# A block order for the value product and one shared tile for the top-k search in a hybrid attention trunk

## The chip, the cores and the metric

The kernel runs on one core of a Trainium2 chip. The metric is the device time of one execution in microseconds. TensorE (PE in the rows, its weight loads PEld) does the matrix products, VectorE (DVE) and ScalarE (ACT) the elementwise work, GpSimd (POOL) part of the copies and splits, SyncE (SP) issues most transfers.

## The reference

One layer over 1024 tokens of width 1024. After an RMS norm, one projection gives the inputs of three groups of heads, whose outputs are joined, multiplied by a SiLU gate, projected back, added to the input and normalised once more. Everything is float32.

```python
# A: differential attention, 6 heads, causal
p = softmax(where(causal, s, NEG)); a = p[:, :, 0] - lam * p[:, :, 1]
o_a = einsum('bhqk,bkhd->bqhd', a, v)
# B: sparse attention, 6 heads over one latent per key; per query the 256 best keys by an index score
rel = relu(einsum('bqhd,bsd->bqhs', iqb, ik))
score = where(causal, einsum('bqhs,bqh->bqs', rel, iwb) * IDX_SCALE, NEG)
_, sel = lax.top_k(score, 256)
o_lat = softmax(qlb . c_kv[sel]) . c_kv[sel];  o_b = einsum('bqhr,hrd->bqhd', o_lat, w_uv)
# C: retention, 4 heads, in chunks of 128
y = silu(gate) * concatenate([o_a, o_b, o_c]);  h = x + y @ w_out;  return rms_norm(h, final_norm)
```

## The kernel before

The 1024 queries are eight blocks of 128, and so are the keys. The work is written as generators that `run` interleaves by weights; within that, a scheduler sets each engine's order when the program is built, from a model of how long instructions take. Where the code stands in a `manual_schedule` block, it keeps the written order on the named engine. On the chip every engine works its queue in order.

The stages, with the times at which they lie in the trace: norm and transposes of x, the projection for keys and values and the index scores (to about 205 us, with TensorE's order written by hand at the end); then, interleaved, differential attention for three pairs of heads (`diff`, two heads each), the top-k search (`topk`) and the remaining projections as filler (to about 548 us); then sparse attention (`dsa`) for query blocks 0 to 3 (to about 612 us) and for blocks 4 to 7 (to about 760 us), with retention and the first output projections as filler; then the last output projections.

`attend` is the frame of `diff` and `dsa`. For each query block i it makes scores (L652 or L717 and L718), a softmax (L663 or L725 with the exponential L665 or L726 on ScalarE), transposes of the weights (L613) that ScalarE or VectorE copies out to the tile `pt` (L113, L117), and, when two query blocks are ready, one value product: a 128x128 result in PSUM whose lower 64 rows (u = 0) belong to query block i-1 and whose upper 64 (u = 1) to block i. Per key block k it is one matmul for each u, except that k = i has u = 1 alone (causal). So a group has 15, 11, 7 or 3 matmuls. There are 48 groups: 24 in differential attention, 12 in each half of sparse attention. A float32 matmul of this kind shows as two records in the trace. The tag "B" has two PSUM buffers, which the transposes and the value products share.

`topk` finds, for each query of blocks 2 to 7, the score that the 256th best key has, bit by bit: per bit, from 30 to 0, it counts how many scores reach a trial threshold. VectorE counts blocks 7, 4 and 2 (`gd`, line L372, with an accumulator), ScalarE blocks 6, 5 and 3 (`ga`, by the sum of a Sign activation, L388). The thresholds of each group stand in a tile of three columns (`tk_cd`, `tk_ca`), the counts in `tk_nd` and `tk_na`, a mask in `tk_md` and `tk_ma`. VectorE turns a count into the next threshold: two instructions for its own group (L394, L395), three for ScalarE's (L397 to L399). The two groups have no data in common until the end, where masks are made from the thresholds (L422 to L432) for sparse attention.

Of the kernel before, what the change touches and what calls it, by code (L numbers as in the profile page):

```python
# [68 lines left out]
class Trunk:  # L69
# [286 lines left out]
    def topk(self):  # L356
# [9 lines left out]
        st = {}  # L366
        thr = self.const("thr", [128, len(ga)])
        for j, b in enumerate(ga):
            nc.vector.memset(thr[:, j:j + 1], float(nv[b] - 2 * TOPK + 1))

        def count(b, t, op, cnt, bit=0):
            nc.vector.tensor_scalar(jv[:, :nv[b]], hb if b == 7 and bit >= 16 else sc[b], t, 0.0, op0=op, op1=OP.add, accum_out=cnt)  # L372

        for key, grp in (("d", gd), ("a", ga)):
            c = self.const("tk_c" + key, [128, len(grp)], I32)
            m = self.const("tk_m" + key, [128, len(grp)], I32)
            cnt = self.const("tk_n" + key, [128, len(grp)])
            st[key] = (c, m, cnt)
            for j, b in enumerate(grp):
                count(b, 0.0, OP.is_ge, cnt[:, j:j + 1])  # L380
            nc.vector.tensor_scalar(m, cnt, float(TOPK), -1.0, op0=OP.is_lt, op1=OP.mult)
            nc.vector.tensor_scalar(c, m, 1 << 30, None, op0=OP.bitwise_xor)
            yield 2.4
        for bit in range(30, -1, -1):
            nxt = (1 << bit) >> 1
            c, m, cnt = st["a"]
            for j, b in enumerate(ga):
                nc.scalar.activation(ja[:, :nv[b]], sc[b], AF.Sign, bias=c[:, j:j + 1].bitcast(F), scale=-1.0,  # L388
                                     accum_out=cnt[:, j:j + 1])
            yield 0.8  # L390
            c, m, cnt = st["d"]
            for j, b in enumerate(gd):
                count(b, c[:, j:j + 1].bitcast(F), OP.is_ge, cnt[:, j:j + 1], bit)
            nc.vector.tensor_scalar(m, cnt, float(TOPK), float(1 << bit), op0=OP.is_lt, op1=OP.mult)  # L394
            nc.vector.scalar_tensor_tensor(c, m, nxt, c, op0=OP.bitwise_xor, op1=OP.bitwise_xor)  # L395
            c, m, cnt = st["a"]
            nc.vector.tensor_tensor(cnt, cnt, thr, OP.is_gt)  # L397
            nc.vector.tensor_scalar(m, cnt, float(1 << bit), float(nxt), op0=OP.mult, op1=OP.add)
            nc.vector.tensor_tensor(c, m, c, OP.bitwise_xor)  # L399
            yield 1.6  # L400
        c, m, cnt = st["a"]
        w = self.const("tk_w", [128, 2, len(ga)])
        for j, b in enumerate(ga):
            count(b, c[:, j:j + 1].bitcast(F), OP.is_gt, cnt[:, j:j + 1])
        cf = c.bitcast(F)
        nc.vector.scalar_tensor_tensor(w[:, 0], cf, -1.0, cf, op0=OP.mult, op1=OP.max)
        nc.vector.tensor_scalar(w[:, 1], cnt, float(TOPK), 2.0 ** -24 * (1 + 2.0 ** -10), op0=OP.is_ge, op1=OP.mult)
# [6 lines left out]
        where = {b: (key, j) for key, grp in (("d", gd), ("a", ga)) for j, b in enumerate(grp)}  # L414
        for b in (7, 6, 5, 4, 3, 2):
            key, j = where[b]
            c, m, cnt = st[key]
            n, T = nv[b], c[:, j:j + 1].bitcast(F)
# [168 lines left out]
    def attend(self, pair, stages, GB=2, groups=(3, 2, 1, 0)):  # L587
# [8 lines left out]
        for t in range(N + 2):  # L596
# [22 lines left out]
            if t >= 2 and steps[t - 2][2] % GB == GB - 1:  # L619
# [354 lines left out]
```

## Time and profile before

| | |
|---|---|
| median of 3 runs | 814.09 us (812.97 to 814.19) |
| the profiled execution | 812.34 us |
| its span in the trace | 810.7 us |
| mean granted TensorE clock | 0.964 of full |
| TensorE, VectorE, ScalarE, GpSimd busy | 743.4, 568.7, 448.1, 332.9 us |
| value product, L627, busy | 78.3 us in 864 records |

Busy time is the time in which an engine has an instruction under way; the ends of matmuls are modelled, so a busy TensorE is not one at its peak, and start-to-start distances tell more than durations. Waits are put down to the engine whose event came last.

### The profile page before, as it was taken

How to read it: one execution, taken by the hardware profiler on the slowest of the kernel's cores; microseconds unless marked ns; L12 is line 12 of the kernel's file. 1: busy time of each engine (PE TensorE's matmuls, PEld its weight loads, DVE VectorE, ACT ScalarE, POOL GpSimd, SP SyncE). 2: the span in 40 equal slices, each digit the busy share in tenths (PEclk: the TensorE clock that was granted, in tenths of full speed). 3: DMA queues.
4: the chain of work that ended last, by engine and by line, in shares of the span. 5: the costliest groups of instructions: out<-in, count | busy, mean ns of one | idle time of the engine just before them, and what ended most of it. 6: DMA issues, size and time to landing. Idle time of an engine off the chain costs nothing.

```text
span 810.7 us, 12950 instructions
## 1 busy us (share of the span) xinstructions
PE 743.4 (92%) x4314; PEld 605.4 (75%) x4314; DVE 568.7 (70%) x1370; ACT 448.1 (55%) x998; POOL 332.9 (41%) x359
## 2 busy tenths in 40 slices
PE   3999999999999989989998789999778999999696
PEld 3798888888778878757876568988546887788584
DVE  5911377899999979999669998354646767653342
ACT  4521455558867857769876556441444656543232
POOL 6403222344424549348647896066745312110000
PEclk9999999999999999989998979999898999999798
DMA  9204644462473253261574573364579845211341
GB/s 331 65 1 106 195 125 145 131 162 84 123 195 101 70 150 109 80 160 34 137 234 143 151 210 116 95 216 144 175 240 300 225 133 166 77 60 59 126 149 59
DMA packets 93186, 113.05 MB, mean 139 GB/s; under 512 B 11840, under 2 KB 63424, under 8 KB 92992
## 3 DMA queue, kind: packets, MB, share of 16 engines
q1 hardware_dynamic: 91824, 109.61, 47.1%
q10 hardware_dynamic: 1296, 2.62, 0.9%
q8 instruction: 34, 0.56, 0.3%
q14 instruction: 32, 0.26, 0.1%
HBM read 75.50 MB, written 36.18 MB: 138 GB/s over the span
## 4 chain that ended last, share of the span: by engine, by line
PE 58%; DVE 23%; DMA 7%; issue 5%; POOL 3%; SPq 2%; ACT 1%; DVEq 0%; ACTq 0%; POOLq 0%
DVE jv L372 7%; PE pB L627 6%; PE pG L132 5%; PE pG L130 5%; PE pG L131 4%; PE pB L613 4%; PE pG L929 4%; PE pG L930 4%; PE pG L931 4%; PE pG L282 3%; PE pG L284 3%; PE pG L283 3%; DVE pp L681 2%; DVE pq L663 2%; PE pS L343 2%
## 5 line engine op out<-in xcount | busy, mean ns | idle before, releaser
L132 PE MATMUL pG<-uh,wl 128*128 128x512 f32 x352 | 143.2, 407 | 1.7 <-POOL wl L123 1.7
L130 PE MATMUL pG<-uh,wh 128*128 128x512 f32 x352 | 143.9, 409 | 0.5 <-POOL wh L119 0.5
L131 PE MATMUL pG<-ul,wh 128*128 128x512 f32 x352 | 143.0, 406 | 0.0
L123 POOL TENSOR_TENSOR wl<-wr,wh 128x512 fp32r<-128x512 f32 x56 | 81.2, 1468 | 115.3 <-PE pG L131 66.4
L388 ACT ACTIVATE ja<-sc,tk_ca 128x896 int8<-128x896 f32 (+2 forms) x93 | 83.3, 896 | 23.6 <-DVE tk_ca L399 9.7
L113 ACT ACTIVATE pt<-pB 128x512 f32<-128x512 f32 (+2 forms) x120 | 58.3, 495 | 56.1 <-PE pB L613 55.9
L613 PE MATMUL pB<-ident,pp 128*128 128x128 f32 x432 | 71.7, 283 | 11.5 <-DVE gt L755 5.4
L132 PEld LDWEIGHTS pG<-uh,wl 128*128 128x128 f32 x352 | 68.1, 194 | 18.1 <-POOL wl L123 2.7
L627 PE MATMUL pB<-pt,v 128*64 128x128 f32 x864 | 78.3, 284 | 2.6 <-ACT pt L113 2.5
L130 PEld LDWEIGHTS pG<-uh,wh 128*128 128x128 f32 x352 | 68.2, 194 | 15.3 <-issue 1.5
L131 PEld LDWEIGHTS pG<-ul,wh 128*128 128x128 f32 x352 | 68.0, 193 | 14.1 <-issue 0.7
L627 PEld LDWEIGHTS pB<-pt,v 128*64 128x64 f32 x864 | 58.8, 139 | 20.8 <-issue 9.1
L678 POOL TENSOR_SCALAR pq<-pq,mx 128x896 f32<-128x896 f32 (+7 forms) x48 | 44.2, 920 | 65.4 <-DVE mx L677 57.9
L613 PEld LDWEIGHTS pB<-ident,pp 128*128 128x128 f32 x432 | 50.7, 142 | 26.0 <-issue 6.5
L372 DVE TENSOR_SCALAR_CACHE_REDUCE jv<-sc,tk_cd 128x640 bf16<-128x640 f32 (+2 forms) x78 | 66.1, 847 | 0.5
L119 POOL TENSOR_SCALAR wh<-wr 128x512 fp32r<-128x512 f32 x56 | 43.4, 780 | 54.4 <-DMA wr<-in_w_in_dram 45.4
L929 PE MATMUL pG<-woh,yh 128*128 128x512 f32 x128 | 52.7, 412 | 11.1 <-ACT yh L113 11.1
L652 PE MATMUL pS<-st,st 128*128 128x512 f32 (+3 forms) x144 | 45.5, 380 | 13.2 <-DVE mx L663 7.0
L282 PE MATMUL pG<-wh,uh 128*128 128x256 f32 x192 | 55.8, 295 | 0.0
L283 PE MATMUL pG<-wl,uh 128*128 128x256 f32 x192 | 55.2, 289 | 0.0
L284 PE MATMUL pG<-wh,ul 128*128 128x256 f32 x192 | 55.0, 288 | 0.0
L345 ACT ACTIVATE pp<-pS 128x1024 f32<-128x1024 f32 (+5 forms) x48 | 36.5, 759 | 31.1 <-PE pS L343 30.5
(226 smaller groups left out, 1794.5 us busy)
## 6 DMA issues: line engine op xcount, KB each, us to landing
wr<-in_w_in_dram SPq DMA_DIRECT2D x56, 256.0 KB, 3.1
st<-qdq SPq DMA_DIRECT2D x24, 256.0 KB, 4.6
st<-qkk SPq DMA_DIRECT2D x18, 256.0 KB, 5.9
x<-in_x_dram SPq DMA_DIRECT2D x8, 512.0 KB, 6.6
qiq<-hl SPq DMA_DIRECT2D x16, 256.0 KB, 3.6
st<-qiq SPq DMA_DIRECT2D x8, 512.0 KB, 3.3
wr<-in_w_out_dram SPq DMA_DIRECT2D x16, 256.0 KB, 4.0
xr<-in_x_dram SPq DMA_DIRECT2D x8, 512.0 KB, 4.2
```

The lines of the kernel that those rows point to most:

```text
L123: (self.nc.vector if e2 == "v" else self.nc.gpsimd).tensor_tensor(lo, src, hi.bitcast(F), OP.subtract)
L130: mm(ps, wh, xh, start=start, stop=False)
L131: mm(ps, wh, xl, start=False, stop=False)
L132: mm(ps, wl, xh, start=False, stop=stop)
L282: mm(ps, uh, hs[k], start=k == 0, stop=False)
L283: mm(ps, uh, ls[k], start=False, stop=False)
L284: mm(ps, ul, hs[k], start=False, stop=k == KC - 1)
L372: nc.vector.tensor_scalar(jv[:, :nv[b]], hb if b == 7 and bit >= 16 else sc[b], t, 0.0, op0=op, op1=OP.add, accum_out=cnt)
L388: nc.scalar.activation(ja[:, :nv[b]], sc[b], AF.Sign, bias=c[:, j:j + 1].bitcast(F), scale=-1.0, accum_out=cnt[:, j:j + 1])
L613: nc.tensor.transpose(p[:, k], pr[:, (k0 + k) * 128:(k0 + k + 1) * 128], self.ident)
L627: nc.tensor.matmul(o[u * 64:(u + 1) * 64], self.v[:, k, h * 64:(h + 1) * 64], pts[g, a][:, k, u * 128:(u + 1) * 128], start=k == 0, stop=k ...
L929: mm(p, yh[:, k - c0], woh[:, k, ds], start=k == c0, stop=False)
```

## The change

Two edits. In `attend`, the matmuls of one value product are put into a `manual_schedule` block for TensorE, so that they keep the written order; that order begins with key block i (u = 1 alone) and goes on with k = 0 to i-1, upper half before lower half. The start and stop flags of the accumulation follow. In `topk`, one tile of six columns each holds all thresholds (`tk_c`), counts (`tk_n`) and masks (`tk_m`), VectorE's three blocks first. VectorE now counts scores below the threshold instead of at or above it, with a constant of its own per column (`thr`), so that the same three updates serve all six columns. Line numbers after the edits are three or four lower than before.

```diff
-        st = {}
-        thr = self.const("thr", [128, len(ga)])
-        for j, b in enumerate(ga):
-            nc.vector.memset(thr[:, j:j + 1], float(nv[b] - 2 * TOPK + 1))
...
+        cols = {b: j for j, b in enumerate(gd + ga)}
+        nd_, nc_ = len(gd), len(cols)
+        thr = self.const("thr", [128, nc_])
+        for b, j in cols.items():
+            nc.vector.memset(thr[:, j:j + 1], nv[b] - TOPK + 0.5 if b in gd else float(nv[b] - 2 * TOPK + 1))
+        c = self.const("tk_c", [128, nc_], I32)
+        m = self.const("tk_m", [128, nc_], I32)
+        cnt = self.const("tk_n", [128, nc_])
...
+        for b in gd + ga:
+            count(b, 0.0, OP.is_ge)
+            yield 0.8
+        nc.vector.tensor_scalar(m, cnt, float(TOPK), -1.0, op0=OP.is_lt, op1=OP.mult)
+        nc.vector.tensor_scalar(c, m, 1 << 30, None, op0=OP.bitwise_xor)
         for bit in range(30, -1, -1):
             nxt = (1 << bit) >> 1
-            c, m, cnt = st["a"]
-            for j, b in enumerate(ga):
-                nc.scalar.activation(ja[:, :nv[b]], sc[b], AF.Sign, bias=c[:, j:j + 1].bitcast(F), scale=-1.0,
-                                     accum_out=cnt[:, j:j + 1])
+            for b in ga:
+                nc.scalar.activation(ja[:, :nv[b]], sc[b], AF.Sign, bias=cut(b), scale=-1.0,
+                                     accum_out=cnt[:, cols[b]:cols[b] + 1])
             yield 0.8
-            c, m, cnt = st["d"]
-            for j, b in enumerate(gd):
-                count(b, c[:, j:j + 1].bitcast(F), OP.is_ge, cnt[:, j:j + 1], bit)
-            nc.vector.tensor_scalar(m, cnt, float(TOPK), float(1 << bit), op0=OP.is_lt, op1=OP.mult)
-            nc.vector.scalar_tensor_tensor(c, m, nxt, c, op0=OP.bitwise_xor, op1=OP.bitwise_xor)
-            c, m, cnt = st["a"]
+            for b in gd:
+                count(b, cut(b), OP.is_lt, bit)
             nc.vector.tensor_tensor(cnt, cnt, thr, OP.is_gt)
             nc.vector.tensor_scalar(m, cnt, float(1 << bit), float(nxt), op0=OP.mult, op1=OP.add)
             nc.vector.tensor_tensor(c, m, c, OP.bitwise_xor)
             yield 1.6
...
                 o = self.pB((128, 128))
                 h = 2 * pair + a
-                for k in range(i + 1):
-                    for u in range(2):
-                        e = i + u - 1
-                        if k <= e:
-                            nc.tensor.matmul(o[u * 64:(u + 1) * 64], self.v[:, k, h * 64:(h + 1) * 64],
-                                             pts[g, a][:, k, u * 128:(u + 1) * 128],
-                                             start=k == 0, stop=k == e, skip_group_check=True)
+                vals = [self.v[:, k, h * 64:(h + 1) * 64] for k in range(i + 1)]
+                with self.tc.manual_schedule(engines={mybir.EngineType.PE}):
+                    for k in (i, *range(i)):
+                        for u in (1, 0):
+                            if k < i or u:
+                                nc.tensor.matmul(o[u * 64:(u + 1) * 64], vals[k], pts[g, a][:, k, u * 128:(u + 1) * 128],
+                                                 start=k == (i if u else 0), stop=k == i - 1, skip_group_check=True)
                 yield 0.5, (a, g, o)
```

TensorE, in sparse attention's first half, around one value product of seven matmuls (pB_6056), before. The rows of L613 are transposes, those of L717 and L718 scores.

```order
L613 MATMUL pB_6044<-ident,pp_6016 128x128 x4
L717 MATMUL pS_6115<-st_6103,st_6101 128x512
L718 MATMUL pS_6115<-st_6105,st_6101 128x512
L627 MATMUL pB_6056<-pt_6029,v_5671 64x128
L717 MATMUL pS_6131<-st_6103,st_6101 128x128
L718 MATMUL pS_6131<-st_6105,st_6101 128x128
L627 MATMUL pB_6056<-pt_6029,v_5671 64x128 x6
L613 MATMUL pB_6077<-ident,pp_6038 128x128
```

The same place after, where the product is pB_6082 (transposes L609, scores L713 and L714):

```order
L609 MATMUL pB_6070<-ident,pp_6039 128x128 x4
L713 MATMUL pS_6147<-st_6135,st_6133 128x512
L714 MATMUL pS_6147<-st_6137,st_6133 128x512
L713 MATMUL pS_6163<-st_6135,st_6133 128x128
L714 MATMUL pS_6163<-st_6137,st_6133 128x128
L624 MATMUL pB_6082<-pt_6055,v_5679 64x128 x7
L609 MATMUL pB_6106<-ident,pp_6064 128x128
```

The value product stood in two pieces of one and six, and stands in one of seven. In the whole order L627 has 78 runs of rows for its 48 groups before, in 39, 20 and 19 for differential attention and the two halves of sparse attention; after, L624 has 48.

VectorE, in a bit of the top-k search in the middle of differential attention, before. L372 counts, L394 and L395 update VectorE's thresholds, L397 to L399 ScalarE's; L123 belongs to a projection.

```order
L372 TENSOR_SCALAR jv,tk_nd<-hb,tk_cd 128x1024
L372 TENSOR_SCALAR jv,tk_nd<-sc_708,tk_cd 128x640
L372 TENSOR_SCALAR jv,tk_nd<-sc_708,tk_cd 128x384
L397 TENSOR_TENSOR tk_na<-tk_na,thr 128x3
L394 TENSOR_SCALAR tk_md<-tk_nd 128x3
L398 TENSOR_SCALAR tk_ma<-tk_na 128x3
L395 SCALAR_TENSOR_TENSOR tk_cd<-tk_md,tk_cd 128x3
L123 TENSOR_TENSOR hl_2189<-pG_2114,hl_2189 128x512
L399 TENSOR_TENSOR tk_ca<-tk_ma,tk_ca 128x3
```

After, at the same head's softmax (L659, L675 to L677):

```order
L377 TENSOR_SCALAR jv,tk_n<-hb,tk_c 128x1024
L377 TENSOR_SCALAR jv,tk_n<-sc_708,tk_c 128x640
L659 ISA pp_1952,mx_1948<-pS_1936,cb 128x896
L659 ISA mx_1948 128x1
L377 TENSOR_SCALAR jv,tk_n<-sc_708,tk_c 128x384
L659 ISA pq_2003,mx_2002<-pS_1987,cb 128x1024
L659 ISA mx_2002 128x1
L396 TENSOR_TENSOR tk_n<-tk_n,thr 128x6
L675 RECIPROCAL mx_1948<-mx_1948 128x1
L397 TENSOR_SCALAR tk_m<-tk_n 128x6
L676 TENSOR_TENSOR mx_1948<-mx_1948,nlam 128x1
L398 TENSOR_TENSOR tk_c<-tk_m,tk_c 128x6
```

Five updates in two chains became three in one, over six columns, and L396 stands behind VectorE's counts and waits for ScalarE's too. Counted over all 31 bits, 28 of the 155 updates of before stand directly in front of the instruction that needs their result; after, 38 of 93.

## Rows read from the trace of the kernel before

**Rows 1.** The page: busy us, share of the span and instructions of each engine.
```profile
PE 743.4 (92%) x4314; PEld 605.4 (75%) x4314; DVE 568.7 (70%) x1370; ACT 448.1 (55%) x998; POOL 332.9 (41%) x359
```

**Rows 2.** Stretches: length, then each engine's busy us, TensorE clock, DMA share, GB/s.
```profile
205.00:420.00 215.00, 203.41 (x1185) 162.86 (x1183) 194.34 (x556) 166.02 (x389) 109.50 (x125) 0.98 0.47 126
420.00:548.00 128.00, 116.63 (x744) 97.21 (x744) 102.65 (x226) 70.21 (x168) 83.42 (x74) 0.93 0.53 155
548.00:612.00 64.00, 50.76 (x340) 38.98 (x339) 31.10 (x103) 22.54 (x64) 39.68 (x50) 0.89 0.64 191
612.00:760.00 148.00, 138.88 (x979) 110.92 (x978) 88.40 (x196) 75.52 (x165) 31.46 (x44) 0.97 0.48 142
```

**Rows 3.** Chain of work: shares by line, 205 to 420; longest pieces, 420 to 548.
```profile
by line: DVE jv L372 18.0%; issue 8.6%; DVE pp L681 8.4%; DVE pq L663 5.1%; PE pG L130 5.1%; PE pG L132 5.0%; PE pG L131 4.9%; DVE pp L663 4.3%; PE pB L627 3.7%; PE pS L652 2.3%; DMA st<-qdk 2.3%; PE pB L613 1.9%; PE pG L284 1.9%; PE pG L28
...
451.48 3.67 POOL wl L123 x2
475.26 4.51 DMA st<-qsq
```

**Rows 4.** TensorE in order of time (start, us, records), around value products.
```profile
205.56 1.97 PE L627 MATMUL pB<-pt,v 128*64 128x128 f32 x30
207.46 0.45 PE L652 MATMUL pS<-st,st 128*128 128x384 f32 x1
...
665.09 1.31 PE L627 MATMUL pB<-pt,v 128*64 128x128 f32 x18
666.33 0.50 PE L717 MATMUL pS<-st,st 128*128 128x512 f32 x1
...
667.15 1.09 PE L627 MATMUL pB<-pt,v 128*64 128x128 f32 x12
668.17 0.55 PE L613 MATMUL pB<-ident,pp 128*128 128x128 f32 x3
```

**Rows 5.** Waits of TensorE, 548 to 612: us in total, times, longest.
```profile
PE pB L613 <- DVE gt L755: 5.4, 2, 4.3
```

**Rows 6.** Waits of TensorE, 300 to 400.
```profile
PE pB L627 <- ACT pt L113: 1.8, 1, 1.8
```

**Rows 7.** ScalarE's groups, 169 to 420: busy us, mean ns | idle before, releaser.
```profile
L388 ACT ACTIVATE ja<-sc,tk_ca 128x896 int8<-128x896 f32 (+2 forms) x93 | 83.3, 896 | 23.6 <-DVE tk_ca L399 9.7 <-DVE tk_ca L382 5.0 <-DVE mx L680 2.9
...
L113 ACT ACTIVATE pt<-pB 128x512 f32<-128x512 f32 (+3 forms) x48 | 22.4, 482 | 4.0 <-PE pB L613 3.9
```

**Rows 8.** VectorE's groups of the top-k search, 169 to 440.
```profile
L372 DVE TENSOR_SCALAR_CACHE_REDUCE jv<-sc,tk_cd 128x640 bf16<-128x640 f32 (+2 forms) x78 | 66.1, 847 | 0.5
L372 DVE TENSOR_SCALAR_CACHE_REDUCE jv<-hb,tk_cd 128x1024 bf16<-128x1024 bf16 x15 | 19.1, 1273 | 0.2
...
L394 DVE TENSOR_SCALAR tk_md<-tk_nd 128x3 int32<-128x3 f32 x31 | 9.0, 290 | 0.2
...
L395 DVE SCALAR_TENSOR_TENSOR tk_cd<-tk_md,tk_cd 128x3 int32<-128x3 int32 x31 | 7.4, 238 | 0.2
```

**Rows 9.** VectorE in order of time (start, us): updates among others, then alone.
```profile
226.25 0.16 DVE L397 TENSOR_TENSOR tk_na<-tk_na,thr 128x3 f32<-128x3 f32 x1
...
226.74 1.27 DVE L372 TENSOR_SCALAR_CACHE_REDUCE jv<-hb,tk_cd 128x1024 bf16<-128x1024 bf16 x1
...
230.06 0.16 DVE L394 TENSOR_SCALAR tk_md<-tk_nd 128x3 int32<-128x3 f32 x1
230.26 0.16 DVE L395 SCALAR_TENSOR_TENSOR tk_cd<-tk_md,tk_cd 128x3 int32<-128x3 int32 x1
```

**Rows 10.** The threshold updates by line: duration ns min/median/max, first and last start.
```profile
L395 DVE SCALAR_TENSOR_TENSOR tk_cd<-tk_md,tk_cd x31: 138/160/1234, 171.0 to 370.4; 128x3 int32<-128x3 int32 x31
L399 DVE TENSOR_TENSOR tk_ca<-tk_ma,tk_ca x31: 139/157/1253, 175.1 to 419.0; 128x3 int32<-128x3 int32 x31
```

**Rows 11.** Waits, 205 to 420.
```profile
DVE tk_na L397 <- ACT ja L388: 9.3, 5, 3.1
ACT ja L388 <- DVE tk_ca L399: 7.9, 8, 3.2
```

More of the change, by code (lines that the diff above doesn't have):

```diff
@@ L365, in topk @@
         nc.gpsimd.tensor_scalar(hb, sc[7].bitcast(BF)[:, 1::2], 1.0, 0.0, op0=OP.mult, op1=OP.add)
-        st = {}
-        thr = self.const("thr", [128, len(ga)])
-        for j, b in enumerate(ga):
-            nc.vector.memset(thr[:, j:j + 1], float(nv[b] - 2 * TOPK + 1))
[L371 to L383, printed above, removed]
+        cols = {b: j for j, b in enumerate(gd + ga)}
@@ new lines, in topk, with count @@
+        nd_, nc_ = len(gd), len(cols)
[5 more added lines that the diff above has]
+        cnt = self.const("tk_n", [128, nc_])
+        def count(b, t, op, bit=0):
+            j = cols[b]
+            nc.vector.tensor_scalar(jv[:, :nv[b]], hb if b == 7 and bit >= 16 else sc[b], t, 0.0, op0=op, op1=OP.add,
+                                    accum_out=cnt[:, j:j + 1])
@@ L384, in topk, with cut @@
+        def cut(b):
+            return c[:, cols[b]:cols[b] + 1].bitcast(F)
+        for b in gd + ga:
[3 more added lines that the diff above has]
+        nc.vector.tensor_scalar(c, m, 1 << 30, None, op0=OP.bitwise_xor)
         for bit in range(30, -1, -1):
             nxt = (1 << bit) >> 1
-            c, m, cnt = st["a"]
-            for j, b in enumerate(ga):
-                nc.scalar.activation(ja[:, :nv[b]], sc[b], AF.Sign, bias=c[:, j:j + 1].bitcast(F), scale=-1.0,
-                                     accum_out=cnt[:, j:j + 1])
+            for b in ga:
+                nc.scalar.activation(ja[:, :nv[b]], sc[b], AF.Sign, bias=cut(b), scale=-1.0,
+                                     accum_out=cnt[:, cols[b]:cols[b] + 1])
@@ L400, in topk @@
             yield 1.6
-        c, m, cnt = st["a"]
         w = self.const("tk_w", [128, 2, len(ga)])
-        for j, b in enumerate(ga):
-            count(b, c[:, j:j + 1].bitcast(F), OP.is_gt, cnt[:, j:j + 1])
-        cf = c.bitcast(F)
+        for b in ga:
+            count(b, cut(b), OP.is_gt)
+        cf = c[:, nd_:].bitcast(F)
         nc.vector.scalar_tensor_tensor(w[:, 0], cf, -1.0, cf, op0=OP.mult, op1=OP.max)
-        nc.vector.tensor_scalar(w[:, 1], cnt, float(TOPK), 2.0 ** -24 * (1 + 2.0 ** -10), op0=OP.is_ge, op1=OP.mult)
+        nc.vector.tensor_scalar(w[:, 1], cnt[:, nd_:], float(TOPK), 2.0 ** -24 * (1 + 2.0 ** -10), op0=OP.is_ge,
+                                op1=OP.mult)
         nc.vector.tensor_tensor(w[:, 0], w[:, 0], w[:, 1], OP.mult)
@@ L413, in topk @@
                      4: C[:, 768:1408], 2: C[:, 1408:1792], 3: T3[:, :512]}
-        where = {b: (key, j) for key, grp in (("d", gd), ("a", ga)) for j, b in enumerate(grp)}
         for b in (7, 6, 5, 4, 3, 2):
-            key, j = where[b]
-            c, m, cnt = st[key]
-            n, T = nv[b], c[:, j:j + 1].bitcast(F)
+            n, T = nv[b], cut(b)
             bias = self.bias[b]
```

## The prediction

> **What bounds the kernel now.** I read the page first, then a table of engine shares by stage, the chain of work and the waits of the longest stage, and last single rows. The profiled execution took 812.34 us, of which the trace spans 810.7; the median of the runs shown is 814.09. TensorE is busy 92% of the span, VectorE 70% [rows 1]. That mean hides two regimes [rows 2]. From 205 to 420 us, where differential attention, the top-k search and the projections run interleaved, TensorE is busy 203.4 of 215 us and VectorE 194.3: both are close to full, and the chain of work in that stretch names VectorE first, the search's counting line L372 with 18.0% [rows 3]. From 612 to 760 us, sparse attention's second half, it is TensorE with 138.9 of 148 us. Between them (420 to 612) no engine is full: the chain's longest pieces there are GpSimd work and transfers [rows 3]. The last 51 us are output projections that neither edit touches. So a saving on VectorE counts before 420 us, one on TensorE counts in full after 612, and in part elsewhere.
>
> **The value product.** The words of the change suggest that alternation is new. It is not: before, the two 64-column halves already alternate, (0,0) (1,0) (0,1) (1,1) and so on, with one matmul over at the end. After, one matmul stands over at the start and the rest alternate; both forms have (n-1)/2 pairs and one single. An uncut group of 15 takes 207.46 - 205.56 = 1.90 us for its 30 records [rows 4], and I expect the same after. What changes is that the group is now one block. Before, the scheduler cut 30 of the 48 groups in two: 78 runs stand in the order for 48 groups, after 48. A cut has a price. A group of 15 in two pieces takes (666.33 - 665.09) + (668.17 - 667.15) = 1.24 + 1.02 = 2.26 us against 1.90, so 0.36 [rows 4]. Each cut adds an entry and an exit, and shifts the pairing so that two more matmuls run alone; pieces of other sizes have the same cause. Thirty cuts are 30 x 0.36 = 10.8 us of TensorE. By loop they are 15 in differential attention, 8 in sparse attention's first half and 7 in its second: 5.4, 2.9 and 2.5 us.
>
> How much lies on the path? In the second half TensorE is 94% busy, so I count all 2.5. In the first half it is busy 50.8 of 64 us [rows 2], and it waits 5.4 us for VectorE's product with the gate [rows 5]; I count half, 1.4. In differential attention it shares the bound with VectorE; half again, 2.7. The edit also adds a wait: the block starts with key block i, the last to be transposed and copied out by ScalarE, so the whole group and all matmuls queued behind it stand until that copy has landed. Before, only the last matmul or two waited. Nearest rows: TensorE sat 1.8 us once from 300 to 400 us for that copy [rows 6]. The cover is the scores, projections and transposes that the scheduler puts between the last transposes and the block. Where the cover is gone the wait is up to one copy, 0.48 us [rows 7]; 48 of these would be 23 us, and none would be 0. I take 0, since the order of after shows scores ahead of the block where the copy could be late, and keep the cost for a rival.
>
> **The top-k updates.** Per bit, VectorE counted three blocks and made five small updates: two for its own blocks, three for ScalarE's. Now one tile holds all six, and three updates serve them: 62 instructions fewer over 31 bits. L394 and L395 were busy 9.0 + 7.4 = 16.4 us [rows 8], which is the upper bound of the gain. But a small update costs what stands around it. From 226.25 to 226.74 us seven small operations of three chains start 0.07 us apart on average, none right behind the one it needs. At 230.06 two that depend on each other, with nothing between, start 0.20 apart [rows 9]. The old form had two independent chains to interleave, the new one has one chain of three. If all old updates had been free (5 x 0.07 = 0.35 us a bit) and all new ones bound (3 x 0.20 = 0.60), the edit would lose 31 x 0.25 = 7.8 us: the other bound. The orders decide between them. Before, 28 of the 155 updates stand directly in front of the one that needs them; after, 38 of 93. That gives 28 x 0.20 + 127 x 0.07 = 14.5 us before and 38 x 0.20 + 55 x 0.07 = 11.4 after: 3 us less, which I take. Busy times longer than that (L394's mean is 290 ns against 0.16 us in quiet rows) are blockages that would, I think, hit the next instruction instead. The first counts lose two small updates, under 0.4 us. The threshold constants are set at the program's start, far ahead of their use: nothing.
>
> The Trainium skill (VectorE: DVE Perf Modes, Rules for kernel authors) holds that chained VectorE operations should be reduced in number, since the flush behind each comes anyway. By that alone the 62 operations would be worth 62 x 0.20 = 12.4 us and the longer chain would cost nothing; the quiet rows, 0.07 against 0.20 us, do not bear it out.
>
> The edit ties two chains. Before, VectorE's own blocks ran ahead: their last update was at 370.4 us, that of ScalarE's blocks at 419.0 [rows 10]. After, each bit ends when the slower side has counted, and L396 waits for ScalarE's third Sign. Queued behind it on VectorE are the softmax steps L659, for whose PSUM tile TensorE waits in turn. Without the short read-outs of the sums, ScalarE needs 3 x 0.896 = 2.7 us a bit and VectorE's three counts (66.1 + 19.1) / 31 = 2.7 [rows 7, 8], so the sides are in balance; with the softmax work that stands between on VectorE it is mostly the later one. So far the wait cost 9.3 us in five places [rows 11]. I take no change and keep its growth as a rival.
>
> **Sum.** 2.7 + 1.4 + 2.5 + 3.0 = 9.6 us. From 812.3 this is 802.7; the median lies 1.8 above the profiled time, so I forecast 804.5 against 814.1.
>
> **Rivals.**
> 1. *Slower: lockstep.* The five waits of 1.9 us for Sign become one in about every second bit: 16 x 1.9 = 30 us, 21 more than before, on a VectorE queue that sets the stretch up to 420 us. Against 9.6 saved that is +11: 825. It decides from about ten such waits, (9.3 + 9.6) / 1.9. For it: ScalarE is busy 166 of 215 us there and its Signs have exponentials and copies between them; and 7.9 us of ScalarE's own waits were for L399 [rows 11], so the loop between the two engines is already felt. Against it: VectorE carries more work per bit than ScalarE. Chance 0.17.
> 2. *No change: the block's head waits.* Each of the 30 groups once cut now stands 0.36 us at its head for the copy, and what the cut cost is paid as idle time; or the stretch from 420 to 612 us absorbs the gain, being set by transfers and GpSimd. The 3 us of VectorE then also vanish into TensorE's own load. 814. For it: TensorE idles little before 420 us. Chance 0.13.
> 3. *More: count alone decides.* Every small update costs 0.20 us whatever stands beside it; 12.4 instead of 3.0 us, and 804.5 - 9.4 = 795. This is where the rule of the Trainium skill would lead. For it: the mean busy times of L394 and L395, 0.29 and 0.24. Against: the 0.07 rows. Chance 0.12.
> 4. *The edit does nothing.* If the pinned block were cut all the same, or alternation were the only point, the 10.8 us would stay. The order shows 48 uncut runs, so this has no chance of its own.
>
> **How the numbers follow.** The forecast (gain between about 4 and 15 us) has 0.58, the rivals 0.17, 0.13 and 0.12. A measurement of this kernel can tell about 0.2%, 1.6 us, from no change. Faster: 0.58 + 0.12 = 0.70, same 0.12, slower 0.18 (a hundredth of rival 2 falls on that side). The range takes rivals 2 and 3 and reaches a little past no change, 793 to 817; what it leaves out is most of rival 1 and the far end of rival 3.
>
> **What would show it.** Right: L624 in 48 runs with 1.90 us for an uncut group of 15 at full clock; 62 update instructions fewer, without longer ones in their place; VectorE's wait for Sign near 9 us; the stretches before 548 us about 6 and after it about 4 us shorter. Wrong: over ten waits of L396 for ScalarE (rival 1), TensorE waits at L624 for the copy beyond some 10 us (rival 2), or a last update of the search much later than 419 us. A reordering of transfers by the scheduler that neither edit asks for could also move the end by a few us; the range has room for it on both sides.

## The result: 790.6 us, and where the time went

The changed kernel takes 790.57 us (788.97 to 792.35, four runs) against 813.53 (812.21 to 814.19, four runs) for the kernel before: 23 us less, a ratio of 0.9734 with a 95% interval of 0.9698 to 0.9769. I had forecast 804.5 with a range of 793 to 817. The direction was right, the size was not, and the time lies under the range. The profiled execution took 791.0 us, of which 789.3 are the span.

The page of the changed kernel, its engines' row (answers to [rows 1]), in busy us, share of the span and instructions:

```profile
PE 721.2 (91%) x4314; PEld 592.3 (75%) x4314; DVE 558.0 (71%) x1311; ACT 448.9 (57%) x996; POOL 329.8 (42%) x359
```

TensorE lost 22.2 us of busy time with the same 4314 records, VectorE 10.7 us with 59 fewer instructions. The four stretches of [rows 2] after the change (length; busy us of TensorE, its weight loads, VectorE, ScalarE, GpSimd; TensorE clock, DMA share, GB/s):

```profile
205.00:420.00 215.00, 199.20 (x1184) 161.44 (x1180) 203.19 (x538) 167.23 (x384) 113.13 (x126) 0.98 0.48 127
420.00:548.00 128.00, 117.10 (x802) 97.89 (x801) 92.16 (x210) 67.42 (x165) 76.96 (x79) 1.00 0.57 167
548.00:612.00 64.00, 54.08 (x394) 42.78 (x392) 41.33 (x121) 30.83 (x79) 39.33 (x47) 0.92 0.79 220
612.00:760.00 148.00, 138.69 (x944) 112.67 (x943) 80.42 (x180) 71.30 (x157) 30.04 (x40) 0.97 0.44 135
```

VectorE is now busy 203.2 of the 215 us up to 420, where it was 194.3, although it has fewer instructions. Fixed times mix up work that has moved, so from here on I cut the span at three points of the work itself, the same in each kernel: the start of the matmul on the sparse scores' first line (L717 before, L713 after) that has number 24 of 72, counted from 0 ("score 24"), and those of numbers 64 and 74 of the 128 on the output projection's first line (L929, L925). First the kernel before, then the changed one, in the same columns (the first window begins at 205 us):

```profile
205.00:603.00 398.00, 365.77 (x2238) 295.66 (x2236) 326.94 (x879) 257.59 (x617) 228.83 (x244) 0.95 0.51 143
603.00:746.20 143.20, 137.47 (x961) 109.24 (x962) 86.19 (x190) 73.54 (x161) 35.22 (x48) 0.98 0.52 153
746.20:764.50 18.30, 10.93 (x55) 8.55 (x54) 3.76 (x10) 4.15 (x9) 0.00 (x0) 0.75 0.44 141
```

```profile
205.00:588.30 383.30, 347.62 (x2226) 284.13 (x2222) 320.48 (x834) 253.96 (x603) 219.05 (x238) 0.98 0.53 147
588.30:725.30 137.00, 134.07 (x970) 108.70 (x971) 84.65 (x190) 74.91 (x163) 40.41 (x52) 0.98 0.56 164
725.30:743.20 17.90, 10.58 (x52) 8.27 (x51) 5.13 (x11) 3.66 (x8) 0.00 (x0) 0.75 0.45 144
```

So 14.7 us were won up to score 24, where I had counted 7.1 (2.7 + 3.0 + 1.4), 6.2 between there and projection 64, where I had counted 2.5, and 0.3 in the third stretch. What the edits did locally is as forecast in one case and not in the other. A value product of 15 matmuls takes 206.10 - 204.21 = 1.89 us, as in [rows 4] (TensorE in order of time):

```profile
204.21 1.96 PE L624 MATMUL pB<-pt,v 128*64 128x128 f32 x30
206.10 0.66 PE L609 MATMUL pB<-ident,pp 128*128 128x128 f32 x4
```

Summed over the program, from a product's first row to the row behind each piece and without waits, the value products held TensorE for 73.3 us before and 62.0 after: 11.3 us less, where the cuts were priced at 10.8. It is not the pin that does this: built without `manual_schedule`, the changed kernel has the same order on all five engines, row for row, and e5 and e6 below keep the pin and have pieces again where they leave out the new order. The product's first matmul now needs the last of the group's copies, so that the whole group becomes ready at once. The search's updates, VectorE from 169 to 440 us, and below the two sides' waits for each other from 205 to 420 (answers to [rows 8] and [rows 11]):

```profile
L396 DVE TENSOR_TENSOR tk_n<-tk_n,thr 128x6 f32<-128x6 f32 x31 | 10.7, 344 | 6.2 <-ACT ja L391 5.5
L397 DVE TENSOR_SCALAR tk_m<-tk_n 128x6 int32<-128x6 f32 x31 | 10.4, 334 | 0.5
L398 DVE TENSOR_TENSOR tk_c<-tk_m,tk_c 128x6 int32<-128x6 int32 x31 | 6.8, 219 | 0.4
```

```profile
ACT ja L391 <- DVE tk_c L398: 12.2, 12, 4.5
...
DVE tk_n L396 <- ACT ja L391: 3.0, 3, 2.0
```

VectorE waits 3.0 us in three places for the Sign, against 9.3 in five before. ScalarE's waits for the thresholds grew from 7.9 to 12.2. The loss by lockstep that rival 1 feared did not come. The last update of the search moved forward, from 419.0 [rows 10] to 397.2 us (start of the last L398):

```profile
L398 DVE TENSOR_TENSOR tk_c<-tk_m,tk_c x31: 139/166/960, 173.1 to 397.2; 128x6 int32<-128x6 int32 x31
```

What an update takes from VectorE is the time from its start to the start of VectorE's next instruction, without waits. Summed over the trace, the 155 updates of before took 31.5 us and the 93 of after 24.3, so 7.2 less. Among them 132 and 77 were quiet (up to 0.4 us long): 14.6 and 10.7 us. The other 23 and 16 were long, up to 1.3 us: 16.9 and 13.6 us. Every long one lay beside a GpSimd instruction that was under way for most of its time, of the quiet ones about one in seven; that GpSimd holds them up was not tested.

### The profile page after: what moved, and what is told of

It is laid out like the page before. It is cut to its first block, busy times and chain, and to the rows that moved or that the text cites. A ratio compares the mean times of both kernels' runs of the same rounds, so it can differ in the third digit from the quotient of the medians.

```text
span 789.3 us, 12915 instructions
## 1 busy us (share of the span) xinstructions
PE 721.2 (91%) x4314; PEld 592.3 (75%) x4314; DVE 558.0 (71%) x1311; ACT 448.9 (57%) x996; POOL 329.8 (42%) x359
## 4 chain that ended last, share of the span: by engine, by line
PE 55%; DVE 19%; DMA 10%; issue 5%; ACT 5%; POOL 4%; SPq 1%; DVEq 0%; ACTq 0%; POOLq 0%
PE pG L130 5%; PE pG L131 5%; PE pG L132 5%; PE pB L624 4%; PE pG L926 4%; PE pG L925 4%; PE pG L927 4%; PE pB L609 3%; PE pG L283 3%; PE pG L284 3%; PE pG L282 3%; DVE jv L377 3%; DVE pp L677 2%; ACT ja L391 2%; PE pS L343 2%
## 5 line engine op out<-in xcount | busy, mean ns | idle before, releaser
L130 PE MATMUL pG<-uh,wh 128*128 128x512 f32 x352 | 141.5, 402 | 0.8 <-DVE vt L117 0.5
L132 PE MATMUL pG<-uh,wl 128*128 128x512 f32 x352 | 139.6, 396 | 0.0
L131 PE MATMUL pG<-ul,wh 128*128 128x512 f32 x352 | 139.4, 396 | 0.0
L123 POOL TENSOR_TENSOR wl<-wr,wh 128x512 fp32r<-128x512 f32 x56 | 80.6, 1454 | 112.9 <-PE pG L131 60.6
L391 ACT ACTIVATE ja<-sc,tk_c 128x896 int8<-128x896 f32 (+2 forms) x93 | 83.4, 896 | 19.2 <-DVE tk_c L398 12.4
L609 PE MATMUL pB<-ident,pp 128*128 128x128 f32 x432 | 72.8, 285 | 6.7 <-DVE f L440 1.6
L130 PEld LDWEIGHTS pG<-uh,wh 128*128 128x128 f32 x352 | 66.4, 189 | 15.0 <-issue 1.3
L132 PEld LDWEIGHTS pG<-uh,wl 128*128 128x128 f32 x352 | 66.3, 188 | 14.9
L377 DVE TENSOR_SCALAR_CACHE_REDUCE jv<-sc,tk_c 128x640 bf16<-128x640 f32 (+4 forms) x81 | 69.1, 854 | 0.8
L609 PEld LDWEIGHTS pB<-ident,pp 128*128 128x128 f32 x432 | 50.5, 143 | 22.9 <-issue 8.2
L624 PE MATMUL pB<-pt,v 128*64 128x128 f32 x864 | 65.2, 287 | 1.3 <-ACT pt L113 1.3
L674 POOL TENSOR_SCALAR pq<-pq,mx 128x896 f32<-128x896 f32 (+7 forms) x48 | 40.6, 846 | 61.1 <-DVE mx L673 49.3
L624 PEld LDWEIGHTS pB<-pt,v 128*64 128x64 f32 x864 | 53.3, 140 | 13.1 <-issue 6.3
L925 PE MATMUL pG<-woh,yh 128*128 128x512 f32 x128 | 52.1, 407 | 7.3 <-ACT yh L113 7.3
L648 PE MATMUL pS<-st,st 128*128 128x512 f32 (+3 forms) x144 | 44.8, 374 | 14.0 <-DVE mx L659 10.6
```

Source lines behind the costliest of these rows:

```text
L123: (self.nc.vector if e2 == "v" else self.nc.gpsimd).tensor_tensor(lo, src, hi.bitcast(F), OP.subtract)
L130: mm(ps, wh, xh, start=start, stop=False)
L131: mm(ps, wh, xl, start=False, stop=False)
L132: mm(ps, wl, xh, start=False, stop=stop)
L391: nc.scalar.activation(ja[:, :nv[b]], sc[b], AF.Sign, bias=cut(b), scale=-1.0, accum_out=cnt[:, cols[b]:cols[b] + 1])
L609: nc.tensor.transpose(p[:, k], pr[:, (k0 + k) * 128:(k0 + k + 1) * 128], self.ident)
```

## Experiments

All runs in one table. "To 24" is the start of score 24 in the profiled run, "24 to P64" the way from there to projection 64, "P64 to 74" the next ten; from projection 74 to the last one (number 127) every kernel needs 36.7 to 37.6 us. wg is a weight in the planner that interleaves attention, search and projections: a change of it leaves every instruction as it is and gives another order. The stretches come from one run each, and the runs of one kernel differ by up to 8.0 us: the profiled run of e1 is the slowest of seven, 4.0 us over their median, that of e12 the slowest of four, 4.3 over, that of e5 the fastest of four, 3.7 under. The ratio is to the runs of the kernel before on the same chip (medians 812.1 to 813.95), with its 95% interval.

| run | value product as a block | search | wg | median us | ratio | to 24 | 24 to P64 | P64 to 74 |
|---|---|---|---|---|---|---|---|---|
| before | no | old | 119 | 813.5 | 1 | 603.0 | 143.2 | 18.2 |
| e13 | no | old | 112 | 796.57 | 0.9790 [0.9759, 0.9821] | 604.8 | 138.8 | 6.9 |
| e9 | no | old | 121 | 796.28 | 0.9814 [0.9767, 0.9861] | 602.6 | 140.1 | 6.9 |
| e14 | no | old | 126 | 824.29 | 1.0127 [1.0095, 1.0159] | 619.1 | 140.5 | 17.8 |
| e1 | both attentions | old | 119 | 806.28 | 0.9925 [0.9896, 0.9953] | 603.5 | 137.3 | 22.0 |
| e7 | no | tied, five updates | 119 | 791.97 | 0.9743 [0.9708, 0.9779] | 598.2 | 139.0 | 6.9 |
| e16 | no | tied, five updates | 112 | 789.73 | 0.9718 [0.9669, 0.9767] | 598.2 | 139.3 | 6.9 |
| e8 | no | separate, three updates | 119 | 787.23 | 0.9682 [0.9640, 0.9724] | 596.8 | 138.7 | 6.9 |
| e17 | no | separate, three updates | 112 | 790.86 | 0.9731 [0.9689, 0.9773] | 598.1 | 139.9 | 6.9 |
| e2 | no | new | 119 | 784.39 | 0.9656 [0.9634, 0.9679] | 589.8 | 141.9 | 6.9 |
| e18 | no | new | 112 | 788.11 | 0.9703 [0.9648, 0.9758] | 592.9 | 140.7 | 6.9 |
| e19 | no | new | 121 | 789.52 | 0.9711 [0.9665, 0.9757] | 594.4 | 139.8 | 6.9 |
| e10 | no | new | 126 | 814.82 | 1.0021 [0.9988, 1.0055] | 609.7 | 139.2 | 18.1 |
| e5 | differential only | new | 119 | 784.77 | 0.9658 [0.9620, 0.9695] | 588.3 | 138.8 | 6.9 |
| e6 | sparse only | new | 119 | 790.25 | 0.9721 [0.9687, 0.9756] | 585.2 | 139.9 | 18.1 |
| after | both | new | 119 | 790.57 | 0.9734 [0.9698, 0.9769] | 588.3 | 137.0 | 18.0 |
| e15 | both | new | 112 | 799.20 | 0.9819 [0.9783, 0.9854] | 592.0 | 134.0 | 22.2 |
| e12 | both | new | 119, nf 1 | 783.00 | 0.9628 [0.9586, 0.9671] | 593.1 | 140.3 | 6.9 |

### The parts apart: e1, e2, e5, e6

Theory 1 held that the cuts of the value product cost more than 10.8 us and the block gives most of the gain, theory 2 that the search edit freed the stretch up to 548 us, theory 3 that the new order as a whole decides and the parts don't add up.

e1_block_alone is the kernel before with the value product's part of the diff only, e2_search_alone with the search's part only:

```diff
-                for k in range(i + 1):
-                    for u in range(2):
...
+                    for k in (i, *range(i)):
+                        for u in (1, 0):
```

```diff
-            nc.vector.tensor_scalar(m, cnt, float(TOPK), float(1 << bit), op0=OP.is_lt, op1=OP.mult)
-            nc.vector.scalar_tensor_tensor(c, m, nxt, c, op0=OP.bitwise_xor, op1=OP.bitwise_xor)
-            c, m, cnt = st["a"]
```

e5_block_diff_only and e6_block_sparse_only are the changed kernel with the new order inside a block in one attention only; the other one's products are ordered as before and lie in pieces again. This is e5, e6 has 2 in place of 4:

```diff
+                first = len(groups) == 4
...
-                    for k in (i, *range(i)):
-                        for u in (1, 0):
+                    for k in ((i, *range(i)) if first else range(i + 1)):
+                        for u in ((1, 0) if first else (0, 1)):
```

> The block order of the value product alone, the top-k search as before. Theory 1 (the cut value products cost more than their 10.8 us of TensorE, because they also held a PSUM buffer and set the order around them): most of the 23 us comes from here, 793 to 799 us. Theory 2 (the search is what freed the stretch up to 420 us): 804 to 809 us, the part of 10.8 us that lies on the path. Theory 3 (the new global order is luck, each edit alone gives something else): anywhere, and the two edits alone do not add up to the whole.

> The shared tile of the top-k search alone, the value product in the order of before. In the built order the value products then stand in 88 runs against 78 before and 48 after. Theory 1: 808 to 814 us, since ten more cuts (3.6 us) eat what the 62 updates saved. Theory 2: 795 to 800 us. Theory 3: 23 us minus this gain differs from the gain of the block alone by more than 5 us.

> Both edits, but the value product keeps the order of before in sparse attention (its 24 groups there are cut again: 68 runs in the whole order). Theory 1: the time lost against the changed kernel is larger than the 20 cuts x 0.36 = 7 us, 8 to 14 us, so 799 to 805 us. Theory 2: at most 4 us lost, 791 to 795. Theory 3: no relation to the number of cuts.

> Both edits, but the value product keeps the order of before in differential attention (71 runs in the whole order, 23 cuts there x 0.36 = 8 us of TensorE). Theory 1: 5 to 12 us lost against the changed kernel, 796 to 803 us. Theory 2: 2 to 4 us lost, since VectorE sets that stretch: 793 to 795 us. Theory 3: no relation to the number of cuts.

Measured: 806.28, 784.39, 784.77 and 790.25 us. The block alone brings about 6 us, the search alone 28, more than the whole change. 6 + 28 is not 23, so something is paid twice or drawn anew. Theory 1 is refuted; theory 2 has the right part, and the time of e1, but for the three kernels with the search edit its ranges were 3 to 11 us too high; theory 3 can't be dismissed. Where the block's gain goes in e1 the waits show. TensorE's largest wait from 205 us to the end of differential attention, first in the kernel before, then in e1, then after (line waited for; us in total, times, longest):

```profile
PE pS L652 <- DVE mx L663: 7.0, 7, 2.4
```

```profile
PE pS L652 <- DVE mx L663: 11.4, 10, 3.8
```

```profile
PE pS L648 <- DVE mx L659: 10.6, 9, 3.0
```

L652 writes the scores into PSUM (L648 after) and must wait until VectorE's softmax step L663 (L659) has read the tile before. With shorter value products TensorE is there earlier and waits 4.4 us more. In e1 score 24 starts at 603.5 us, in the kernel before at 603.0: up to there these two runs show no gain from the block. As the profiled run of e1 was a slow one, a gain of up to 4 us is not ruled out.

### Fewer updates or tied chains: e7, e8

The search edit does two things: it issues three updates in place of five, and it ties VectorE's own blocks to ScalarE's. e7 ties and has five (two idle ones behind the three), e8 has three and doesn't tie. In e8 one update in place of three lies on the way from one Sign to the next, so it doesn't tell a shorter way from fewer updates:

```diff
 # e7, on e2
             nc.vector.tensor_tensor(c, m, c, OP.bitwise_xor)
+            nc.vector.tensor_scalar(c, c, 0, None, op0=OP.bitwise_xor)
+            nc.vector.tensor_scalar(c, c, 0, None, op0=OP.bitwise_xor)
 # e8, on the kernel before
-            nc.vector.tensor_tensor(cnt, cnt, thr, OP.is_gt)
-            nc.vector.tensor_scalar(m, cnt, float(1 << bit), float(nxt), op0=OP.mult, op1=OP.add)
-            nc.vector.tensor_tensor(c, m, c, OP.bitwise_xor)
+            nc.vector.scalar_tensor_tensor(c, cnt.bitcast(I32), 0, c, op0=OP.bitwise_and, op1=OP.bitwise_xor)
```

> The search edit alone (value product as in the kernel before) came out at 784.4 us against 812.6. Here it has its lockstep (one tile, VectorE's blocks wait for ScalarE's counts) but two idle updates of the thresholds follow the three in every bit, so that it issues five per bit again, as the kernel before does: 62 instructions, about 12 us of VectorE, come back. Theory count (the saved updates are the gain): 806 to 812. Theory lockstep (the gain is that the counts of VectorE's own blocks no longer run ahead, so the softmax work of differential attention gets VectorE earlier): 784 to 792. Theory order (the scheduler's new order of everything else is the gain, and any edit draws another one): no forecast from the mechanism, anywhere from 780 to 815.

> The kernel before with its two separate tiles, so no lockstep, and three updates per bit in place of five: ScalarE's blocks get one update that waits for their counts and leaves their threshold as it is (so these three blocks search with a fixed threshold: their rows come out with other picks, with the same instructions behind). Theory count: 784 to 792, as the search edit alone. Theory lockstep: 805 to 812, as the kernel before less a few us. Theory order: anywhere from 780 to 815.

Measured: 791.97 and 787.23 us. Neither pure theory survives: each half alone brings most of the 28 us, so again the sum is off. One reason is in the table: both, like e2, have the short stretch from projection 64 to 74, which the kernel before has not. The next runs show where it comes from.

### The same instructions in another order: e9, e10, e13, e14

Only the planner's weight differs, on the kernel before (e9 121, e13 112, e14 126) and on e2 (e10 126):

```diff
-'wg': 119
+'wg': 121
```

> The kernel before with one weight of its planner changed by under 2% (wg 121 for 119): the same instructions, in another order in 617 rows of TensorE's program. Theories count and lockstep: 810 to 816, since no work changes. Theory order: more than 6 us away from the kernel before in either direction.

> The search edit alone with the same weight changed (wg 126 for 119): the same instructions as the run at 784.4 us, in another order in 620 rows of TensorE's program. Theories count and lockstep: 782 to 788. Theory order: more than 6 us away from 784.4, most likely upward, since 784.4 was the best of six draws.

Measured: 796.28 and 814.82 us. The kernel before gains 16 us, and the search edit loses 30, with not one instruction more or less. So a single pair of orders can't price an edit here. The stretches of the table bring order into this: between score 24 and projection 64 all kernels need 134 to 143 us, and the ten projections from 64 to 74 need either 6.9 us or 17.8 to 22.2, never a value between. TensorE in order of time there, in the changed kernel (start, us, records; in brackets the wait):

```profile
729.54 1.52 PE L624 MATMUL pB<-pt,v 128*64 128x128 f32 x22
738.38 0.79 PE L925 MATMUL pG<-woh,yh 128*128 128x512 f32 x1 [7.32 <-ACT yh L113]
738.97 0.63 PE L926 MATMUL pG<-wol,yh 128*128 128x512 f32 x1
...
743.67 0.63 PE L926 MATMUL pG<-wol,yh 128*128 128x512 f32 x1
744.09 0.52 PE L927 MATMUL pG<-woh,yr 128*128 128x512 f32 x1
744.46 0.40 PE L925 MATMUL pG<-woh,yh 128*128 128x512 f32 x1
```

and in e2, where the last value product stands in two pieces:

```profile
720.37 1.31 PE L623 MATMUL pB<-pt,v 128*64 128x128 f32 x18
...
722.73 0.65 PE L623 MATMUL pB<-pt,v 128*64 128x128 f32 x4
723.31 0.50 PE L925 MATMUL pG<-woh,yh 128*128 128x512 f32 x1
723.64 0.39 PE L926 MATMUL pG<-wol,yh 128*128 128x512 f32 x1
```

In the changed kernel, as in the kernel before, 174 projection matmuls stand behind the last value product, and the first of them needs what that product gives: TensorE waits 7.3 us for ScalarE's copy yh, which itself waited 4.1 us for the transfer that brings the gated product (yr from yd). Then TensorE runs some 5 us at 0.43 us from start to start in place of 0.23: the granted clock from 738.38 to 743.67 is 0.50, the lower level of 1.2 GHz. In e2 and e9 228 stand there, and the first 54 don't need that product; they fill the way. Of the 11 us between the two kinds, 7.3 are the stop, 2.3 the lower clock, and 1.5 the last value product itself, which in e2 and e9 lies ahead of projection 64. So the stretches from score 24 to 64 and from 64 to 74 share out the work differently in the two kinds. Which of the two an order has can be read from the built program without running it.

> The kernel before with wg 112 for 119: the same instructions, 746 rows of TensorE's order differ. 228 projection matmuls stand behind the last value product, so theory tail expects 796 to 804, as the reordered kernel before at 796.3. If the order scatters without such a rule: anywhere from 785 to 830.

> The kernel before with wg 126 for 119: the same instructions, 362 rows of TensorE's order differ, and 174 projection matmuls stand behind the last value product, as in the kernel before. Theory tail: 809 to 817. If the order scatters without such a rule: anywhere from 785 to 830.

Measured: 796.57 us, as the tail theory said from the 228 in its order; and 824.29, 7 us above its range. The tail of e14 was as said (17.8 us); the miss is up to score 24, at 619.1. That is 16 us later than the other three orders of the old search, and e10, with the same weight of 126, is 17 us later than the other orders of the new one. This weight costs as much with either search; by which waits stays open.

### The tail alone, and the whole change in another order: e12, e15

e12 is the changed kernel with one row block of the projection fewer among the filler of sparse attention's second half; TensorE's order is the same for the first 3876 of its 4314 records, far behind score 24. e15 is the changed kernel with the weight 112:

```diff
-'nf': 2
+'nf': 1
 # e15
-'wg': 119
+'wg': 112
```

> The changed kernel with one number of its planner changed (nf 1 for 2): one row block of the output projection instead of two is offered as filler beside sparse attention's second half. The order differs only in the last tenth: 219 projection matmuls stand behind the last value product instead of 174, of which the first 45 don't need that product. In the traces so far kernels with 174 there stood 17.9 to 22 us in the stretch from projection 64 to 74 (TensorE waits for the last heads' output, then runs at a lower granted clock), kernels with 228 only 7. Theory tail (this wait is a matter of the order alone, 11 us): 778 to 782, which would beat every kernel so far. Theory block (in sparse attention the block order itself makes the last product late and costs 6 us): 788 to 792.

> The changed kernel with wg 112 for 119: the same instructions, 573 rows of TensorE's order differ, 174 projection matmuls behind the last value product as in the changed kernel. If the gain of 23 us is the edits' own work: 788 to 794. If it is a lucky order, as the 30 us between the two orders of the search edit suggest: above 797.

Measured: e12 783.00 us (780.07 to 787.34), 7.6 less than the changed kernel and 1 us over the range of theory tail. The third stretch fell from 18.0 to 6.9 us, at full granted clock:

```profile
733.40:740.30 6.90, 6.90 (x31) 5.67 (x30) 2.72 (x6) 2.14 (x7) 0.00 (x0) 1.00 0.52 149
```

The block stands in sparse attention here as it does in the changed kernel, so the long tail doesn't come with the block, and its 11 us are more than the 6 between e5 and e6. In the profiled runs the whole fell by 3.7 us, from 791.0 to 787.3: score 24 came 4.9 us later (593.1 against 588.3) on the same order of TensorE up to there, and the next stretch took 3.3 more, with the last value product in it. So one look at one order is good to no better than 5 us up to score 24. e15 came at 799.20, with a tail of 22.2. With weight 112 before and after, the change as a whole would have read 796.57 to 799.20: no gain. Up to projection 64 e15 is 17.5 us ahead of e13; its tail gives 15.2 of them back.

### A second order for each corner: e16 to e19

e16 is e7 and e17 is e8 with weight 112; e18 and e19 are e2 with 112 and 121.

> Tied chains with five updates per bit (two of them idle), in another order (wg 112 for 119; 287 rows of TensorE differ, 228 projection matmuls behind the last value product). Square theory (fewer updates about 7 us, tied chains about 6, additive): score 24 of sparse attention at 596 to 600 us after the start, median 790 to 794. Only fewer updates count: score 24 at 601 to 605, median 795 to 799. Scatter of the order: elsewhere.

> Three updates per bit on two separate chains (ScalarE's three blocks search with a fixed threshold), in another order (wg 112 for 119; 300 rows of TensorE differ, 228 projection matmuls behind the last value product). Square theory: score 24 at 595 to 599 us, median 785 to 790. Only tied chains count: score 24 at 601 to 605, median 794 to 799. Scatter of the order: elsewhere.

> The search edit alone in another order (wg 112 for 119; 215 rows of TensorE differ, 228 projection matmuls behind the last value product). Square theory: score 24 at 588 to 592 us, median 783 to 787. Scatter of the order: score 24 beyond 595.

> The search edit alone in a third order (wg 121 for 119; 475 rows of TensorE differ, 228 projection matmuls behind the last value product). Square theory: score 24 at 588 to 592 us, median 783 to 787. Scatter of the order: score 24 beyond 595, as with wg 126, where it came at 609.7.

Measured: 789.73, 790.86, 788.11 and 789.52 us. To score 24 they need 598.2, 598.1, 592.9 and 594.4 us: the first two as the square theory said, the last two 1 and 2 us over its range but short of 595; the whole times lie up to 3 us outside of theirs. Mean start of score 24 without the weight 126:

| | separate chains | tied chains |
|---|---|---|
| five updates | 603.5 (603.0, 604.8, 602.6) | 598.2 (598.2, 598.2) |
| three updates | 597.5 (596.8, 598.1) | 592.4 (589.8, 592.9, 594.4) |

Both rows and both columns agree: 62 updates fewer bring 5.8 to 6.0 us, the tie 5.1 to 5.3. The whole times of the same kernels, without the kernel before and its long tail, average 796.4, 790.9, 789.0 and 787.3 us (five separate, five tied, three separate, three tied). Here 62 updates fewer bring 7.4 on separate chains and 3.5 on tied ones, the tie 5.6 with five updates and 1.7 with three, where the medians of the two corners overlap. With the weight 126 the search edit brings 619.1 - 609.7 = 9.4, near the 11.1 of the square. In whole times with equal tails it is 8.5 us (e13 to e18), 6.8 (e9 to e19) and 9.5 (e14 to e10). To score 24 the steps of 5 to 6 us stand against a spread of up to 2.2 us within three corners and 4.6 in the fourth, and no two neighbouring corners overlap. So that either half counts is shown; that they are equal, or that they add up, is not.

Why the tie helps can be seen on VectorE, from 320 us on in windows of 60 us (length, busy us): first the kernel before, then the changed one, then e7.

```profile
320.00:380.00 60.00, 59.17 (x155) 0.94 0.37 98
380.00:440.00 60.00, 45.54 (x116) 0.95 0.56 163
```

```profile
320.00:380.00 60.00, 56.44 (x144) 0.94 0.35 96
380.00:440.00 60.00, 57.47 (x137) 0.97 0.62 172
```

```profile
320.00:380.00 60.00, 58.51 (x148) 0.97 0.37 99
380.00:440.00 60.00, 56.50 (x149) 1.00 0.53 150
```

Before, VectorE has a hole of 14.5 us from 380 to 440: its own blocks were done at 370.4 us [rows 10], and the search ran on alone on ScalarE. VectorE's longest wait from 370 to 440 us (in total, times, longest) is for that search; the rest are mostly waits for TensorE and for other work of ScalarE:

```profile
DVE tk_na L397 <- ACT ja L388: 6.9, 4, 3.1
```

The hole is no matter of one order: it has 11.3 to 20.8 us in the five kernels with the old search, and 2.5 to 7.0 in the thirteen others. With the tie VectorE's counts are spread out to the end, and the softmax work gets VectorE earlier. The counts' own share shows the move (instructions on the tile jv, 205 to 320 us, before, after, e7):

```profile
205.00:320.00 115.00, 47.74 (x104) 0.99 0.48 127
```

```profile
205.00:320.00 115.00, 44.60 (x97) 1.00 0.49 129
```

```profile
205.00:320.00 115.00, 37.92 (x84) 1.00 0.47 126
```

In e8, which doesn't tie, the hole is gone as well (VectorE is busy 56.4 us from 380 to 440): with one update in place of three between two Signs, ScalarE's last Sign starts at 388 us and not at 418. Both halves thus close the same hole from its two ends; that this is all they do was argued, not shown.

## Why the prediction was wrong

**The size of the search edit, the term that failed most.** I put 3.0 us on fewer updates. For quiet updates the prices came near: on the mean I had 0.09 us for one of before and 0.12 for one of after, and the trace has 0.11 and 0.14. The step that failed is the one on the long updates, "blockages that would, I think, hit the next instruction instead". They went with the updates, 23 to 16, and took 3.3 us less; and where e7 has 62 idle updates more than e2, 20 long ones became 35. On VectorE this makes 7.2 us. The square has 5.8 to 6.0 of it up to score 24, 0.10 us for each of the 62 updates, twice my net price. The bound of 16.4 us by busy time was farther off on the other side. Rival 3 (795) came nearest in time, but its price of 0.20 each was not borne out. The Trainium skill (VectorE: DVE Perf Modes, Rules for kernel authors) says to reduce the number of chained operations; these runs agree with the direction, at half of the price that I had worked out from it.

**The tie, put at nothing, with a loss for its rival.** "I take no change and keep its growth as a rival": it brought 5 us up to score 24, and 1.7 to 5.6 in the whole times. I had read that VectorE's blocks ran ahead [rows 10] and asked only what waits would grow. The question I left out was what VectorE does once it has run ahead: it stands idle for a quarter of the 60 us from 380 on, in a stretch where it is otherwise nearly full. My table of stretches [rows 2] ended its first row at 420 and averaged this hole into 194.3 of 215.

**The value product.** The 10.8 us of TensorE are right to within 0.5 (73.3 to 62.0), and so is the count of 48 runs. For sparse attention's second half I counted 2.5. From score 24 to projection 64 the four kernels with the block in sparse attention and the long tail need 137.1 us on the mean, the three without the block 141.0; with the short tail it is 140.3 for e12 and 139.7 for the ten without. So 2.5 is neither shown nor refuted. Of "half again, 2.7" for differential attention and 1.4 for the first half e1, on the old search, shows nothing up to score 24, and its waits for VectorE's softmax grew by 4.4 us. With the new search the five kernels with a block average 589.4 there, the three without (but for weight 126) 592.4, so 3.0, less than the scatter of a single look. Rival 2 (the copy at the block's head) was not it: TensorE waits 1.3 us in two places at L624 for the copy.

**What I did not count: the order.** I granted "a reordering of transfers" a few us. The order of the whole program is drawn anew by any edit, and it is worth 16 us between e9 and before, 30 between e2 and e10, of which the stretch at the program's end has 11. The changed kernel did not even draw the short tail.

**Sum by measured terms**, for the profiled runs, 21.4 us of span. Up to score 24 it is 14.7: 11.1 for the search and 3.0 for the block, where I had 3.0 and 4.1. Behind score 24 it is 6.2, where I had 2.5, and the 143.2 us of the kernel before are the longest of all eighteen there. Of the 11.8 us that my 9.6 lacked, the search makes up 8.1; the other 3.7 can't be told from the luck of this order against that one. On a single order I could not have known them, and the tail might as well have added or taken 11. A range down to 780 would have been honest.

**What is open.** Why the weight 126 costs 16 us with either search, whether the two halves of the search edit add up, why some updates are long, and how much of the block's gain is real. The faster versions found are e12 (783.0), e2 (784.4) and e5 (784.8); their intervals overlap, and each is faster than both kernels.

## To carry to other kernels

Where a planner sets the order, first run the kernel before in two or three orders with the same instructions: their scatter is the smallest effect that one comparison can show, and stretches cut at points of the work help to tell an edit from a reordering, as long as the same work lies between the points. Where two engines share a search, look for a hole on the bound engine after its own part has ended; tying the two can be worth more than the wait it adds. At the end of a program, count what stands behind the last product that doesn't need it.

## What I had not expected of the hardware

A stop of 7.3 us on TensorE cost some 10 us and not 7. Behind it the projection matmuls start 0.43 us apart for about 5 us, at a granted clock of 0.50 (1.2 GHz), before they come back to 0.23; that is 2.8 us more than at 0.23 throughout (the rows of the tail above). And a small VectorE operation of 0.16 us in quiet surroundings was worth 0.10 us up to score 24 when 62 of them went, and as much when 62 idle ones were put back. The 62 idle ones took 15.4 us from VectorE (40.8 in e7 against 25.4 in e2) and moved score 24 by 5.8: neither the spacing of a quiet row nor the sum of busy times is the price.
